# Scaling attention A's probabilities on GpSimd instead of DVE, in two operations for each head

## The chip, the core and the metric

The kernel runs on one core of one Trainium2 chip. The metric is the device time of one execution in microseconds (us). A core has TensorE (PE, with its weight loads as PEld), VectorE (DVE), ScalarE (ACT), GpSimd (POOL) and SyncE (SP), each with its own instruction stream that it works through in order, and 16 DMA engines.

## What is computed

Two layers of an encoder over 256 tokens of width 1024, all in float32. Each layer has three token mixers that read one common projection, and a gated MLP with a short convolution. The mixer that matters here is A, attention over all 256 tokens with 8 query heads and 2 key/value heads of width 64:

```python
q = rmsnorm(q.reshape(B, S, A_HEADS, HEAD_DIM), gq)
k = rmsnorm(k.reshape(B, S, A_KV_HEADS, HEAD_DIM), gk)
q = rope_2d(q, row, col) * (HEAD_DIM ** -0.5)
k = rope_2d(k, row, col)
s = jnp.einsum('bqkgd,bskd->bkgqs', qi, k).astype(jnp.float32)
p = jax.nn.softmax(s, axis=-1)
o = jnp.einsum('bkgqs,bskd->bqkgd', p, v)
```

The other mixers are B, average pooling over windows of 2, 4, 8 and 16 tokens minus the token itself, with a linear map, and C, attention over a neighbourhood on a grid.

## The kernel before

Every large product is made of three float32r products: each operand is split into a part `hi` and a remainder `lo`, and `mm3` (lines 204 to 206) adds hi x hi, lo x hi and hi x lo in PSUM. The weights come from HBM in chunks of 128 x 1024 (`raw`, issued by SP, line 154); ACT rounds each half chunk to `hi` (line 163) and DVE subtracts to get `lo` (line 168; GpSimd does it for some chunks of the MLP). `feed` keeps up to six split chunks ahead of TensorE.

In a layer, first the projections for A are made and q and k normed and rotated (`prep_a`). The rotation uses tables `rt` that hold cosine and sine multiplied by the gains of the q/k norm. `rope_tables` (lines 316 to 326) makes them on GpSimd: for each of the two gains two small copies (line 323) and four products of 128x64 (lines 325 and 326), so 12 instructions for a layer. The gains `gq` of layer 2 are loaded by SP (line 304). In the code `load_qk` and `rope_tables` for layer 2 are called in the middle of layer 1's MLP, but a scheduler sets the order of each engine's instructions by priority and by when it expects operands, and it has put both far earlier, into layer 1's attention.

Then the projections for B and C are computed, and the heads of A are laid between them. `attend` (line 582) makes one step of A for each block of a projection. A step n transposes the probabilities of head n-2 (`turn`, line 504), computes the scores of head n (lines 481 and 482), multiplies finished pairs of heads with v (`pv`, line 514), and after that block calls `scale` for head n. The softmax of a head h is:

- DVE takes the negated maximum over the keys, straight from PSUM (line 484), and multiplies it with the norm of q (line 485).
- ACT computes the exponentials into an SBUF tile `e` of 128 x 2 x 256, one instruction for each half of 128 queries, which also sums them (line 489).
- DVE takes the reciprocals of the two sums (line 495) and multiplies all of `e` by them (line 496).
- TensorE transposes `e` in four pieces (line 504), ACT copies the result from PSUM (line 506), and line 514 multiplies it with v.

Between the heads DVE also does the pooling sums of B (lines 609 to 621) and the weight splits (line 168). After the last head GpSimd issues 16 DMAs that spread C's values (line 672).

In the names, `w` stands for the tiles of `w2` and `w1`, `st` for small statistics, `ps` for a PSUM bank, `big` for the tiles of 128 x 1088, `y` for what the branches give. The lines that the change touches are 495 and 496:

```python
dve.reciprocal(rc, sm)
dve.tensor_tensor(e, e, rc[:, :, None].to_broadcast([128, 2, S]), op=OP.mult)
```

Of the kernel before, what the change touches and what calls it, by code (L numbers as in the profile page):

```python
# [13 lines left out]
OP = mybir.AluOpType  # L14
# [4 lines left out]
S = 256  # L19
# [56 lines left out]
def encoder(ctx: ExitStack, tc: tile.TileContext, x, norms, wall, bgate, gqk, wpool, pscale,  # L76
            rpbt, convp, rope, inv, out):
    nc = tc.nc
    pe, act, dve, pool = nc.tensor, nc.scalar, nc.vector, nc.gpsimd
# [19 lines left out]
    def st(n=1):  # L99
        return sb.tile([128, 16], FT, name="st", bufs=16)[:, :n]  # L100
# [107 lines left out]
    def split_from(o_hi, o_lo, src, scale=None):  # L208

        if scale is None:  # L210
            a = act.activation(o_hi, src, AF.Copy)
            b = dve.tensor_tensor(o_lo, src, o_hi, op=OP.subtract)  # L212
        else:
            a = act.activation(o_hi, src, AF.Copy, scale=scale)
            b = dve.scalar_tensor_tensor(o_lo, src, scale, o_hi.bitcast(FT), op0=OP.mult, op1=OP.subtract)
        return a, b
# [130 lines left out]
    for l in range(L):  # L347
# [124 lines left out]
        class AttA:  # L472
# [19 lines left out]
            def scale(self, h):  # L492
                e, sm = self.P[h]
                rc = st(2)
                dve.reciprocal(rc, sm)
                dve.tensor_tensor(e, e, rc[:, :, None].to_broadcast([128, 2, S]), op=OP.mult)

            def turn(self, h):
                e, _ = self.P.pop(h)
# [457 lines left out]
```

## Time and profile before

| | before |
|---|---|
| median of 3 runs | 830.1 us (829.84 to 830.25) |
| profiled execution | 830.15 us |
| its span, first to last instruction | 828.1 us |
| PE busy | 813.2 us (98%) |
| PEld busy | 708.7 us (86%) |
| DVE busy | 598.8 us (72%) |
| ACT busy | 505.4 us (61%) |
| POOL busy | 109.1 us (13%) |
| granted TensorE clock, mean | 0.998 |

The profile is of one execution. Its busy times are sums over the whole span; a wait is idle time of an engine, put down to what ended it; the timeline gives each engine's instructions in order of time, in us from the start of the span, and puts equal neighbours together. A duration there runs until the result is written, so that neighbours on an engine overlap by some hundredths of a microsecond.

### The profile page before, as it was taken

The page shows a single profiled execution, that of the slowest core. Times are in us where ns is not written, and L with a number is a line of the kernel's source. Part 1 is how long each engine was busy: PE and PEld are TensorE (multiplying, and loading weights), DVE is VectorE, ACT ScalarE, POOL GpSimd, SP SyncE. Part 2 cuts the span into 40 slices and gives each one's busy share as a digit, 9 for nine tenths or more (in the row PEclk, how much of TensorE's full clock was granted, in tenths as well). Part 3 has the DMA queues.
Part 4 walks back from the last instruction along what each step waited for, and adds up shares of the span by engine and source line. Part 5 has one row for each costly group of instructions (what it writes and reads, how often), then busy time and mean ns, then how long its engine had stood idle before and what let it go on. Part 6 is the DMA issues. An engine that isn't in the chain of part 4 may idle for free.

```text
span 828.1 us, 13731 instructions
## 1 busy us (share of the span) xinstructions
PE 813.2 (98%) x5016; PEld 708.7 (86%) x5016; DVE 598.8 (72%) x1172; ACT 505.4 (61%) x1072; POOL 109.1 (13%) x133
## 2 busy tenths in 40 slices
PE   8999999999999999999999999999999999999997
PEld 6898787887789999999889887888787899999995
DVE  5898566776668876667689965776667598766673
ACT  6667555555558755565567765655446686556652
POOL 3221400000011212111021004000001212121100
PEclk9999999999999999999999999999999999999999
DMA  8874557566575665566356535466654746655521
GB/s 290 296 262 128 166 189 241 169 196 194 167 244 182 201 200 180 177 185 197 110 201 226 173 110 153 166 214 218 205 176 133 241 161 193 188 193 182 180 98 51
DMA packets 44580, 153.90 MB, mean 186 GB/s; under 512 B 5985, under 2 KB 6241, under 8 KB 44258
## 3 DMA queue, kind: packets, MB, share of 16 engines
q1 hardware_dynamic: 43488, 150.94, 56.1%
q0 software_dynamic: 1024, 2.10, 0.9%
q8 instruction: 39, 0.64, 0.3%
q14 instruction: 27, 0.22, 0.1%
q10 hardware_dynamic: 2, 0.00, 0.0%
HBM read 149.87 MB, written 1.05 MB: 182 GB/s over the span
## 4 chain that ended last, share of the span: by engine, by line
PE 84%; DVE 7%; issue 2%; POOL 2%; DMA 2%; ACT 2%; SPq 1%; DVEq 0%; POOLq 0%; ACTq 0%
PE ps L204 27%; PE ps L205 26%; PE ps L206 26%; DVE lo L168 2%; DMA gq<-in_gqk 1%; POOL st L223 1%; PE ps L514 1%; DVE big L250 1%; PE ps L504 1%; DVE x L270 1%; ACT hi L163 1%; PE ps L563 1%; DMA raw<-in_wall 1%; PE ps L530 1%; DVE hTlo L212 1%
## 5 line engine op out<-in xcount | busy, mean ns | idle before, releaser
L163 ACT ACTIVATE hi<-raw 128x512 fp32r<-128x512 f32 x528 | 310.8, 624 | 117.7 <-PE ps L205 43.0
L168 DVE TENSOR_TENSOR lo<-raw,hi 128x512 fp32r<-128x512 f32 x486 | 323.0, 691 | 79.6 <-ACT hi L163 77.0
L204 PE MATMUL ps<-hThi,hi 128*128 128x256 f32 x768 | 218.1, 284 | 0.0
L206 PE MATMUL ps<-hThi,lo 128*128 128x256 f32 x768 | 217.0, 283 | 0.0
L205 PE MATMUL ps<-hTlo,hi 128*128 128x256 f32 x768 | 216.9, 282 | 0.0
L204 PEld LDWEIGHTS ps<-hThi,hi 128*128 128x128 f32 x768 | 146.9, 191 | 2.3 <-issue 0.8
L205 PEld LDWEIGHTS ps<-hTlo,hi 128*128 128x128 f32 x768 | 146.9, 191 | 1.7
L206 PEld LDWEIGHTS ps<-hThi,lo 128*128 128x128 f32 x768 | 146.9, 191 | 0.0
L204 PE MATMUL ps<-hi,hThi 128*128 128x512 f32 (+1 forms) x352 | 136.5, 390 | 0.0
L205 PE MATMUL ps<-lo,hThi 128*128 128x512 f32 (+1 forms) x352 | 134.8, 385 | 0.9 <-DVE lo L168 0.8
L206 PE MATMUL ps<-hi,hTlo 128*128 128x512 f32 (+1 forms) x352 | 134.9, 385 | 0.4 <-DVE hTlo L212 0.4
L204 PE MATMUL ps<-hi,y 128*128 128x512 f32 x272 | 108.7, 399 | 0.0
L205 PE MATMUL ps<-lo,y 128*128 128x512 f32 x272 | 107.6, 395 | 0.0
L206 PE MATMUL ps<-hi,y 128*128 128x512 f32 x272 | 107.6, 395 | 0.0
L168 POOL TENSOR_TENSOR lo<-raw,hi 128x512 fp32r<-128x512 f32 x42 | 55.9, 1352 | 238.1 <-ACT hi L163 238.1
L205 PEld LDWEIGHTS ps<-lo,hThi 128*128 128x128 f32 x352 | 67.2, 191 | 14.2 <-DVE lo L168 2.0
L206 PEld LDWEIGHTS ps<-hi,hTlo 128*128 128x128 f32 x352 | 67.1, 191 | 14.3 <-DVE hTlo L212 2.0
L204 PEld LDWEIGHTS ps<-hi,hThi 128*128 128x128 f32 x352 | 67.2, 191 | 14.0 <-issue 1.1
L833 ACT ACTIVATE w<-ps,cvp 128x256 f32<-128x256 f32 x88 | 48.2, 556 | 35.4 <-DVE w L835 35.4
L206 PEld LDWEIGHTS ps<-hi,y 128*128 128x128 f32 x272 | 51.1, 188 | 12.4
L204 PEld LDWEIGHTS ps<-hi,y 128*128 128x128 f32 x272 | 51.3, 188 | 11.8 <-issue 1.1
L834 DVE SCALAR_TENSOR_TENSOR w<-ps,cvp,w 128x255 f32<-128x255 f32 x88 | 41.8, 479 | 26.9 <-ACT w L833 26.7
(130 smaller groups left out, 840.8 us busy)
## 6 DMA issues: line engine op xcount, KB each, us to landing
raw<-in_wall SPq DMA_DIRECT2D x264, 512.0 KB, 3.9
gb<-in_bgate SPq DMA_DIRECT2D x12, 256.0 KB, 5.2
rpbt<-in_rpbt SPq DMA_DIRECT2D x2, 1024.0 KB, 6.5
gpost<-in_norms SPq DMA_DIRECT2D x4, 512.0 KB, 6.7
vb<-w POOLq DMA_DIRECT2D x32, 64.0 KB, 2.6
gpre<-in_norms SPq DMA_DIRECT2D x3, 512.0 KB, 4.3
out_x<-x SPq DMA_DIRECT2D x4, 256.0 KB, 2.0
x<-in_x SPq DMA_DIRECT2D x2, 256.0 KB, 3.2
```

Of the source, the lines that this page charges most:

```text
L163: act.activation(hi[c][:, z], raw[c][:, z], AF.Copy)
L168: (pool if lean else dve).tensor_tensor(lo[c][:, z], raw[c][:, z], hi[c][:, z], op=OP.subtract)
L204: pe.matmul(o, a[0], b[0], start=first, stop=False)
L205: pe.matmul(o, a[0], b[1], start=False, stop=False)
L206: pe.matmul(o, a[1], b[0], start=False, stop=last)
L212: b = dve.tensor_tensor(o_lo, src, o_hi, op=OP.subtract)
L223: pool.tensor_tensor(r, v, mhalf[:, :1], op=OP.pow)
L250: par["xn"] = dve.scalar_tensor_tensor(xn[:, c], xs[t][:, c], r, g[h], op0=OP.mult, op1=OP.mult)
L270: dve.scalar_tensor_tensor(xs[t][:, c], mg[:, c], r, xs[t][:, c], op0=OP.mult, op1=OP.add)
L504: pe.transpose(p3[:, k, t * 128:(t + 1) * 128], e[:, t, k * 128:(k + 1) * 128], ident)
L833: act.activation(u[:, c:c + S], p[:, c:c + S], AF.Identity, bias=cvp[:, l, j, 3:4], scale=cvp[:, l, j, 1:2])
L834: dve.scalar_tensor_tensor(u[:, c + 1:c + S], p[:, c:c + S - 1], cvp[:, l, j, 0:1], u[:, c + 1:c + S], op0=OP.mult, op1=OP.add)
```

## The change

The reciprocal stays on DVE. The multiplication of `e` becomes two GpSimd operations, one for each half of 128 queries, each with one tensor operand of 128 x 256 and one column of `rc` as the scalar of each partition. Lines from 496 on have a number one higher in the changed kernel, and the new operation is line 497.

```diff
                 e, sm = self.P[h]
                 rc = st(2)
                 dve.reciprocal(rc, sm)
-                dve.tensor_tensor(e, e, rc[:, :, None].to_broadcast([128, 2, S]), op=OP.mult)
+                for t in range(2):
+                    pool.tensor_scalar(e[:, t], e[:, t], rc[:, t:t + 1], None, op0=OP.mult)
```

The scheduler places the new operations. On GpSimd, in layer 1's attention, the order before was this (L400 belongs to `prep_a`, L323 to L326 are the rotary tables of layer 2, L672 the DMAs of C's values):

```order
L400 TENSOR_TENSOR rq<-st,mhalf 128x8
L323 COPY gq<-gq 128x2x16 x2
L325 TENSOR_TENSOR rt<-ropec,gq 128x64 x2
L326 TENSOR_TENSOR rt<-ropec,gq 128x64 x2
L323 COPY gq<-gq 128x2x16 x2
L325 TENSOR_TENSOR rt<-ropec,gq 128x64 x2
L326 TENSOR_TENSOR rt<-ropec,gq 128x64 x2
L672 DMA vb<-w_1059 32x512 x2
```

With the change the same place of GpSimd's queue reads (L497 is the scaling, one row for the two halves of a head):

```order
L400 TENSOR_TENSOR rq<-st,mhalf 128x8
L497 TENSOR_SCALAR w_680<-w_680,st 128x256 x2
L323 COPY gq<-gq 128x2x16 x2
L325 TENSOR_TENSOR rt<-ropec,gq 128x64 x2
L326 TENSOR_TENSOR rt<-ropec,gq 128x64 x2
L323 COPY gq<-gq 128x2x16 x2
L325 TENSOR_TENSOR rt<-ropec,gq 128x64 x2
L326 TENSOR_TENSOR rt<-ropec,gq 128x64 x2
L497 TENSOR_SCALAR w_730<-w_730,st 128x256 x2
L497 TENSOR_SCALAR w_787<-w_787,st 128x256 x2
L497 TENSOR_SCALAR w_848<-w_848,st 128x256 x2
```

Head 0 stands ahead of the 12 rotary instructions, heads 1 to 7 behind them and ahead of the DMAs. In layer 2 the eight heads follow each other with nothing between.

On DVE, from the reciprocal of head 0 in layer 1 on, the order before was this (L612 to L621 are the pooling sums):

```order
L495 RECIPROCAL st<-st 128x2
L484 TENSOR_REDUCE st<-ps 128x2
L496 TENSOR_TENSOR w_680<-w_680,st 128x512
L485 TENSOR_TENSOR st<-st,rq 128x2
L613 TENSOR_TENSOR big<-big 128x257
L168 TENSOR_TENSOR lo<-raw,hi 128x512 x2
L495 RECIPROCAL st<-st 128x2
L621 TENSOR_TENSOR w_924<-w_924,big 128x256
L496 TENSOR_TENSOR w_729<-w_729,st 128x512
L484 TENSOR_REDUCE st<-ps 128x2
L620 TENSOR_TENSOR w_927<-big,invc 128x256
L485 TENSOR_TENSOR st<-st,rq 128x2
```

With the change, from the same reciprocal on (the pooling sums have numbers one higher):

```order
L495 RECIPROCAL st<-st 128x2
L484 TENSOR_REDUCE st<-ps 128x2
L614 TENSOR_TENSOR big<-big 128x257
L485 TENSOR_TENSOR st<-st,rq 128x2
L168 TENSOR_TENSOR lo<-raw,hi 128x512 x2
L622 TENSOR_TENSOR w_928<-w_928,big 128x256
L495 RECIPROCAL st<-st 128x2
L621 TENSOR_TENSOR w_931<-big,invc 128x256
L621 TENSOR_TENSOR w_991<-big,invc 128x256
L622 TENSOR_TENSOR w_931<-w_931,big 128x256
L168 TENSOR_TENSOR lo<-raw,hi 128x512
L484 TENSOR_REDUCE st<-ps 128x2
```

The scalings are gone, and the pooling products have moved up into their places. TensorE's and SP's orders are the same as before, ACT's differs by one exchange of neighbours, and outside the heads of attention A DVE's is the same too.

## Rows read from the trace of the kernel before

**Rows 1.** The page, part 1: busy time, share of the span and instructions.

```profile
PE 813.2 (98%) x5016; PEld 708.7 (86%) x5016; DVE 598.8 (72%) x1172; ACT 505.4 (61%) x1072; POOL 109.1 (13%) x133
```

**Rows 2.** TensorE's waits: line, waited for: us in total, times, longest.

```profile
PE ps L504 <- DVE st L485: 2.7, 2, 1.5
```

**Rows 3.** Groups by form, DVE: count, busy us, mean ns, idle before.

```profile
L496 DVE TENSOR_TENSOR w<-w,st 128x512 f32<-128x512 f32 x16 | 11.1, 696 | 0.3
```

**Rows 4.** Timeline of DVE, layer 1: start us, us, instruction, count.

```profile
56.49 0.16 DVE L495 RECIPROCAL st<-st 128x2 f32<-128x2 f32 x1
56.56 0.67 DVE L484 TENSOR_REDUCE st<-ps 128x2 f32<-128x512 f32 x1
57.15 0.68 DVE L496 TENSOR_TENSOR w<-w,st 128x512 f32<-128x512 f32 x1
...
58.16 1.29 DVE L168 TENSOR_TENSOR lo<-raw,hi 128x512 fp32r<-128x512 f32 x2
59.36 0.16 DVE L495 RECIPROCAL st<-st 128x2 f32<-128x2 f32 x1
...
59.76 0.68 DVE L496 TENSOR_TENSOR w<-w,st 128x512 f32<-128x512 f32 x1
...
63.57 0.81 DVE L496 TENSOR_TENSOR w<-w,st 128x512 f32<-128x512 f32 x1
```

**Rows 5.** Timeline of TensorE, layer 1: transposes of heads 0, 1 and 2.

```profile
57.98 0.63 PE L504 MATMUL ps<-ident,w 128*128 128x128 f32 x4 [1.13 <-DVE st L485]
...
61.80 0.60 PE L504 MATMUL ps<-ident,w 128*128 128x128 f32 x4
...
65.59 0.60 PE L504 MATMUL ps<-ident,w 128*128 128x128 f32 x4
```

**Rows 6.** Timeline of GpSimd, layer 1: first four and last two of 12 rotary instructions.

```profile
57.81 2.70 POOL L323 COPY gq<-gq 128x32 f32<-128x32 f32 x2 [19.42 <-DMA gq<-in_gqk]
60.48 0.60 POOL L325 TENSOR_TENSOR rt<-ropec,gq 128x64 f32<-128x64 f32 x2
...
64.53 0.78 POOL L326 TENSOR_TENSOR rt<-ropec,gq 128x64 f32<-128x64 f32 x2
```

**Rows 7.** Timeline of GpSimd, start of layer 1: its own 12, first and last two.

```profile
14.93 0.35 POOL L323 COPY gq<-gq 128x32 f32<-128x32 f32 x2 [3.13 <-DMA gq<-in_gqk]
...
17.67 1.57 POOL L326 TENSOR_TENSOR rt<-ropec,gq 128x64 f32<-128x64 f32 x2
```

**Rows 8.** GpSimd's forms: ns min/median/max, L600 as a group with mean ns.

```profile
L323 POOL COPY gq<-gq x8: 203/305/1704, 14.9 to 62.6; 128x32 f32<-128x32 f32 x8
L139 POOL MEMSET klo<- x1: 529/529/529, 0.9 to 0.9; 128x512 f32 x1
L600 POOL MEMSET big<- 128x32 f32 x2 | 0.2, 124 | 7.4 <-DVE big L394 6.5 <-PE ps L405 0.8
L168 POOL TENSOR_TENSOR lo<-raw,hi x42: 1287/1302/1497, 246.8 to 787.2; 128x512 fp32r<-128x512 f32 x42
```

**Rows 9.** Timeline of DVE, layer 2: reciprocal and scaling of head 0, scaling of head 1.

```profile
461.75 0.15 DVE L495 RECIPROCAL st<-st 128x2 f32<-128x2 f32 x1
461.82 0.67 DVE L484 TENSOR_REDUCE st<-ps 128x2 f32<-128x512 f32 x1
462.41 0.68 DVE L496 TENSOR_TENSOR w<-w,st 128x512 f32<-128x512 f32 x1
...
465.28 0.68 DVE L496 TENSOR_TENSOR w<-w,st 128x512 f32<-128x512 f32 x1
```

**Rows 10.** Timeline of TensorE, layer 2: transposes of heads 0 and 1.

```profile
463.24 0.63 PE L504 MATMUL ps<-ident,w 128*128 128x128 f32 x4 [1.54 <-DVE st L485]
...
467.05 0.60 PE L504 MATMUL ps<-ident,w 128*128 128x128 f32 x4
```

**Rows 11.** Groups by form, GpSimd: the DMAs of attention C's values.

```profile
L672 POOL DMA_DIRECT2D vb<-w x32 | 17.5, 550 | 82.0 <-ACT w L668 80.9 <-DMA vb<-w 1.2
```

**Rows 12.** Stretch of layer 1's heads: length, PE, PEld, DVE, ACT, POOL busy, PEclk, DMA.

```profile
53.00:92.00 39.00, 37.87 (x264) 33.36 (x263) 31.39 (x70) 28.19 (x72) 7.50 (x12) 1.00 0.49 155
```

## The prediction

> **What bounds the kernel now.** I read the page's busy times first. TensorE is busy for 813.2 of the span's 828.1 us [rows 1], so almost all of the time is TensorE's own stream, which is in order and which the change leaves as it is. The only time that the change can give or take is what TensorE waits. So the second view is TensorE's waits: of the few it has, the largest are two before the transposes of attention A's probabilities (line 504), 2.7 us together, the longer one 1.5 [rows 2]. They are the first head of each layer. The trace names L485 as the releaser, the small DVE instruction right behind the scaling; what the transposes read is the tile that the scaling wrote.
>
> The third view is the order in time of DVE and TensorE around the heads. In layer 1 head 0's reciprocal starts at 56.49, the maximum of the next head (L484) stands between, and the scaling runs from 57.15 to 57.83 [rows 4]; the transposes start at 57.98 [rows 5], 0.15 later, which I take as the price of a hand-over. Head 1 is scaled by 60.44 and turned at 61.80: 1.36 to spare. Head 2 is scaled by 64.38 and turned at 65.59: 1.21 to spare [rows 4, 5]. In layer 2 head 0 is scaled by 463.09 and turned at 463.24, with nothing to spare; head 1 by 465.96 and 467.05, 1.09 to spare [rows 9, 10]. So a scaling that ends more than about 1.1 us later stops TensorE, and what TensorE stops for is not won back: after these heads its stream has nearly no waits that could shrink.
>
> The fourth view is GpSimd in that stretch, and it decides the case. At 57.81, when the DMA of the next layer's q/k gains lands, GpSimd begins that layer's rotary tables, and it is busy with those 12 small instructions until 65.31 [rows 6]. This is in the midst of heads 1 and 2.
>
> **The change part by part.** *Removed:* 16 DVE operations of 0.696 us, 11.1 in all [rows 3]. DVE is busy for 31.39 of the 39 us of layer 1's heads [rows 12], TensorE does not wait for DVE's weight splits there, and so this relief is worth nothing by itself. What it could bring is an earlier scaling for the two heads that TensorE waits for, below.
>
> *Added: 32 GpSimd operations of 128x256.* No row has this one. The nearest is the copy of 128x32, also with one operand of a tensor: 0.203 us at its shortest. The two sizes of memset, 124 ns for 32 and 529 for 512 elements, give 0.84 ns for each element; 224 more elements make 0.19, so 0.39 us [rows 8]. The other end is the subtraction of two tensors, 1.302 us for 512 elements, so 0.65 for half of it [rows 8]. I take 0.40, since it is one tensor and a scalar, and 0.80 for a head. The Trainium skill (GPSIMD Engine Reference, sections 3.1 and 4.1) says that operations with one input run at about the rate of the port, 1.03 cycles for each element, which makes an estimate of 0.22 us for each half; by that the sum below would be 0.36 us smaller. The trace of before has no such operation.
>
> *What GpSimd pays for DVE's neighbourhood.* The two copies at 57.81 take 2.70 us instead of some 0.4 [rows 6, 8]: while they stand there DVE runs subtractions and multiplications that read two tensors of SBUF, from L168 at 58.16 to the scaling that ends at 60.44 [rows 4], and the next pair of GpSimd instructions takes only 0.60 [rows 6], under the maximum of head 2, which reads PSUM. So GpSimd waits while DVE reads two SBUF tensors and runs freely when it does not. The first half of a scaling meets the L484 that follows the reciprocal, the second one an L168 or the like.
>
> *Moved: the place in GpSimd's queue.* The order shows head 0's halves ahead of the 12 rotary instructions in layer 1 and head 1's behind them, with every later head behind those. So head 1's scaling, which DVE did at 59.76, starts only when the tables are through. How long do they take now? At the start of layer 1 its own 12 took from 14.93 to 19.24, 4.31 us, with DVE less crowded [rows 7]; here 7.50 [rows 6]. In the changed order DVE still runs the pooling sums and the weight splits around them, but not the scalings, two of which (0.60 each from start to start) fell into this run. I take 7.5 - 1.2 = 6.3 us, so up to 57.81 + 6.3 = 64.1. Head 1 then needs 0.80, and 0.3 for a DVE operation under way: 65.2; with 0.15 for the hand-over its transposes start at 65.36 instead of 61.80. **That is 3.56 us of standing TensorE.**
>
> *The other heads.* Behind head 1 the queue has nothing but scalings. From a reciprocal to the end of the scaling DVE took 1.08 (59.36 to 60.44 [rows 4]); GpSimd takes 0.15 + 0.80 and up to two waits of 0.60, so 0.95 to 2.15, at worst 1.07 more, and the smallest spare time is 1.09: hidden. Head 0 of layer 2: the reciprocal ends at 461.90, the first half runs 462.05 to 462.45, under L484. The second half either follows at once (TensorE at 463.00, a gain of 0.24) or waits for the L168 that now starts where the scaling did, at 462.41 (463.56, a loss of 0.32) [rows 9, 10]. I take 0. Head 0 of layer 1 is the same, and its gain or loss vanishes in the longer wait for head 1. The DMAs of attention C's values stand behind the last scaling on GpSimd's queue, and waited 80.9 us for ACT's copies [rows 11]: they have time.
>
> *Sum.* 3.56 + 0 + 0, rounded to 3.5. The profiled execution took 830.15 us, 0.05 above the median of 830.1, so 830.15 + 3.5 = 833.6 us. Low end: tables at the pace of layer 1's own end at 62.12, the transposes start at 63.37, a loss of 1.57, less 0.24: 831.5; with every duration at its shortest (4 copies of 0.203, 8 products of 0.30: 3.2 us, no waits) the loss is 0.2 and the time 830.1. High end: head 0's second half is held until the next reciprocal (59.36), the tables start 2.0 later and take 7.5, the halves cost 0.65 and two waits: 69.96, a loss of 8.16, and 0.32 in layer 2: 838.6.
>
> **The rivals.** *1. The tables get through in time.* Decisive is when the 12 instructions end: by 62.5 the loss stays under 1.7 us. For it: their own durations are 3.2 us, layer 1's own took 4.3, three scalings are gone from DVE, and when TensorE stops DVE runs dry and lets GpSimd through. Against it: DVE's new order packs the pooling products closer together here. Time: 830.1 to 831.5, say 831.0, which is not slower by what can be told.
>
> *2. The clock falls in the stop.* At the heads no stop so far is longer than 1.5 us [rows 2], and the granted clock is 1.00 across the heads [rows 12]. A stop of 3.5 us or more has no row. Should the clock drop to 1.2 GHz, the products of one head (57.98 to 61.80, 3.8 us [rows 5]) would take up to twice as long: 833.6 + 3.8 = 837.4. The Trainium skill (TensorE: Matmul & The Clock Gate, Part 1) calls the lower level the default, which comes back when TensorE idles; no row here bears it out.
>
> *3. GpSimd is starved at every head.* If a half costs 0.65 and each half waits out several DVE operations, heads 1 and 2 of both layers come late by a further 1 to 2 us each: 836 to 839. Against it: from head 3 on DVE has idle time in each period, 7.6 of 39 us in all [rows 12].
>
> *4. Faster.* The two waits of 2.7 us [rows 2] could go if the scaling of both first heads came much earlier. It cannot come earlier than the reciprocal, which leaves some 0.2 each. As a case only what I overlook: 827.5 to 828.4.
>
> **How the numbers follow.** The forecast, GpSimd held up at head 1, loss of 1.7 to 5.5: 0.70. Rival 1: 0.15. Rivals 2 and 3 together: 0.12. Rival 4: 0.03. About 0.2% (1.7 us) is what a measurement of this kernel can tell from no change. So slower 0.82, same 0.15, faster 0.03. The range from 830.6 to 837.0 takes in most of rival 1, the forecast with its bounds, and half of rivals 2 and 3.
>
> **What would show it.** In the profile after: a wait of TensorE before line 505 (504 before) of about 3.5 us near 61 to 65 us, released by GpSimd, and none like it in layer 2; the tables' 12 instructions from about 57.8 to 64; 32 GpSimd operations whose shortest is near 0.40; DVE's busy time down by about 11 us; a granted clock of 1.00 from 53 to 100 us. Wrong would be: the transposes of head 1 at 62 or 63 (rival 1), waits at line 505 in several heads (rival 3), matmuls twice as far apart behind the stop (rival 2).

## The result, and the profile after

The changed kernel took **836.61 us** (median of 6 runs, 836.03 to 838.53) beside 829.97 us for the kernel before in the same session: a ratio of 1.0084, 95% interval 1.0074 to 1.0095. So it is 6.6 us slower. The profiled execution took 836.47 us with a span of 834.5 (828.1 before), so 6.4 us of span are to be found. The transposes are L505 in the changed kernel.

The page's busy times of the changed kernel, to be read against [rows 1]:

```profile
PE 816.2 (98%) x5016; PEld 711.0 (85%) x5016; DVE 590.4 (71%) x1156; ACT 506.5 (61%) x1072; POOL 140.1 (17%) x165
```

DVE has lost 8.4 us and GpSimd has gained 31, for 32 instructions. TensorE does the same 5016 instructions and is busy 3.0 us longer, which points to a slower clock; the rest of the 6.4 must be waits. TensorE's waits (line, waited for: us in total, times, longest), against [rows 2]:

```profile
PE ps L505 <- POOL w L497: 6.0, 4, 3.5
```

Four waits in place of two, 6.0 us in place of 2.7, and one of 3.5. The timeline of TensorE in layer 1 shows where, against [rows 5] (start us, us, instruction, count, idle before and its releaser):

```profile
57.75 0.33 PE L505 MATMUL ps<-ident,w 128*128 128x128 f32 x1 [0.90 <-POOL w L497]
61.62 0.90 PE L505 MATMUL ps<-ident,w 128*128 128x128 f32 x3 [3.54 <-POOL w L497]
...
67.75 0.60 PE L505 MATMUL ps<-ident,w 128*128 128x128 f32 x4
...
71.53 0.60 PE L505 MATMUL ps<-ident,w 128*128 128x128 f32 x4
```

It is head 0, not head 1. Its first piece, which reads the first half of the scaling, runs at 57.75, 0.23 earlier than before; the other three wait for the second half until 61.62 (57.98 before): **3.64 us lost**. Head 1 does not wait at all, and yet it comes 5.95 us later than before (67.75 against 61.80), so another **2.31 us** went between the two heads, where TensorE never stood still. Head 2 is 5.94 late: nothing is added behind head 1.

The 2.31 us are the clock. Windows of two microseconds (window, length, busy us of PE, PEld, DVE, ACT and POOL, granted clock PEclk, DMA share, GB/s), against [rows 12], where it was 1.00:

```profile
56.00:58.00 2.00, 1.10 (x9) 0.79 (x7) 2.00 (x7) 2.00 (x6) 1.24 (x2) 1.00 0.81 183
58.00:60.00 2.00, 0.08 (x1) 0.00 (x0) 2.00 (x7) 1.98 (x6) 2.00 (x1) 1.00 0.53 184
60.00:62.00 2.00, 0.38 (x2) 0.38 (x3) 0.86 (x2) 0.00 (x0) 2.00 (x4) 0.55 0.63 242
62.00:64.00 2.00, 2.00 (x11) 2.00 (x10) 0.59 (x1) 1.12 (x2) 2.00 (x9) 0.50 0.03 8
64.00:66.00 2.00, 2.00 (x12) 2.00 (x11) 1.97 (x6) 1.01 (x3) 2.00 (x3) 0.50 0.23 39
66.00:68.00 2.00, 2.00 (x15) 2.00 (x15) 0.27 (x2) 0.25 (x3) 2.00 (x3) 0.74 0.63 223
68.00:70.00 2.00, 2.00 (x20) 2.00 (x18) 1.15 (x2) 2.00 (x4) 0.99 (x2) 1.00 0.00 0
```

TensorE stood from 58 to 61.6, the granted clock fell to 0.50 (1.2 of 2.4 GHz) near 60, and it was back at 1.00 only near 67. In between, the products start 0.21 us apart instead of 0.12, and 11 or 12 instructions stand in a window that holds 20 at the full clock (68 to 70).

Why did the second half come so late? GpSimd (against [rows 6]) and DVE (against [rows 4]) in the changed kernel:

```profile
56.76 4.80 POOL L497 TENSOR_SCALAR w<-w,st 128x256 f32<-128x256 f32 x2 [19.09 <-DVE st L495]
61.52 0.35 POOL L323 COPY gq<-gq 128x32 f32<-128x32 f32 x2
...
63.81 1.07 POOL L326 TENSOR_TENSOR rt<-ropec,gq 128x64 f32<-128x64 f32 x2
```

```profile
56.50 0.16 DVE L495 RECIPROCAL st<-st 128x2 f32<-128x2 f32 x1
56.58 0.67 DVE L484 TENSOR_REDUCE st<-ps 128x2 f32<-128x512 f32 x1
57.16 0.42 DVE L614 TENSOR_TENSOR big<-big 128x257 f32<-128x257 f32 x1
57.50 0.15 DVE L485 TENSOR_TENSOR st<-st,rq 128x2 f32<-128x2 f32 x1
57.57 1.28 DVE L168 TENSOR_TENSOR lo<-raw,hi 128x512 fp32r<-128x512 f32 x2
58.77 0.42 DVE L622 TENSOR_TENSOR w<-w,big 128x256 f32<-128x256 f32 x1
59.11 0.16 DVE L495 RECIPROCAL st<-st 128x2 f32<-128x2 f32 x1
59.18 0.74 DVE L621 TENSOR_TENSOR w<-big,invc 128x256 f32<-128x256 f32 x2
59.84 0.42 DVE L622 TENSOR_TENSOR w<-w,big 128x256 f32<-128x256 f32 x1
60.17 0.68 DVE L168 TENSOR_TENSOR lo<-raw,hi 128x512 fp32r<-128x512 f32 x1
63.41 0.69 DVE L484 TENSOR_REDUCE st<-ps 128x2 f32<-128x512 f32 x1 [2.55 <-PE ps L482]
```

The two halves take 4.80 us together, until 61.56. The first starts under the maximum L484, which reads PSUM, and takes 0.93. The second is ready at 57.7, when DVE has begun a row of ten instructions without a gap, all but the reciprocal with two operands from SBUF. That row ends at 60.85. By the group of L497 a half costs 0.92 us where nothing stands against it:

```profile
L497 POOL TENSOR_SCALAR w<-w,st x32: 917/927/3885, 56.8 to 496.3; 128x256 f32<-128x256 f32 x32
```

Counted back from its end, 61.56, these 0.92 begin at 60.64, 0.2 us before the end of DVE's row. It reads as if the half had hardly run before. Neither ScalarE nor the DMA explains this: the first half took its plain 0.93 in the window from 56 to 58, with ACT busy for all 2.00 us and a DMA share of 0.81, while in the next window, where the second half does not come through, they stand at 1.98 and 0.53. Then DVE has nothing to do until TensorE makes new scores (2.55 us idle), so the rotary tables behind it run almost freely: 61.52 to 64.88, 3.4 us.

In layer 2 the halves are late once more, by little: head 1 is turned at 473.23 (6.18 later than in [rows 10]), and head 2 at 477.35 (470.84 before, 6.51 later), so layer 2 adds 6.51 - 5.94 = 0.57. The sum is 3.64 + 2.31 + 0.57 = 6.5, against 6.4 of span.

### The profile page after: what moved, and what is told of

It is laid out like the page before. It is cut to its first block, busy times and chain, and to the rows that moved or that the text cites. A ratio compares the mean times of both kernels' runs of the same rounds, so it can differ in the third digit from the quotient of the medians.

```text
span 834.5 us, 13759 instructions
## 1 busy us (share of the span) xinstructions
PE 816.2 (98%) x5016; PEld 711.0 (85%) x5016; DVE 590.4 (71%) x1156; ACT 506.5 (61%) x1072; POOL 140.1 (17%) x165
## 4 chain that ended last, share of the span: by engine, by line
PE 84%; DVE 7%; POOL 2%; issue 2%; ACT 2%; DMA 1%; DVEq 0%; POOLq 0%; ACTq 0%
PE ps L204 26%; PE ps L205 26%; PE ps L206 26%; DVE lo L168 3%; DVE big L250 1%; POOL st L223 1%; PE ps L515 1%; ACT hi L163 1%; POOL w L497 1%; PE ps L505 1%; DVE x L270 1%; DMA raw<-in_wall 1%; PE ps L564 1%; PE ps L531 1%; DVE hTlo L212 1%
## 5 line engine op out<-in xcount | busy, mean ns | idle before, releaser
L168 DVE TENSOR_TENSOR lo<-raw,hi 128x512 fp32r<-128x512 f32 x486 | 323.9, 692 | 87.9 <-ACT hi L163 84.0
L168 POOL TENSOR_TENSOR lo<-raw,hi 128x512 fp32r<-128x512 f32 x42 | 55.9, 1353 | 238.1 <-ACT hi L163 238.1
L223 POOL TENSOR_TENSOR st<-st,mhalf 128x1 f32<-128x1 f32 x16 | 11.4, 714 | 342.4 <-DVE st L233 342.4
```

The source lines that it names most:

```text
L168: (pool if lean else dve).tensor_tensor(lo[c][:, z], raw[c][:, z], hi[c][:, z], op=OP.subtract)
L223: pool.tensor_tensor(r, v, mhalf[:, :1], op=OP.pow)
```

## The experiments

Two theories stood after this. **Held half:** the second half of head 0 is passed over while DVE runs its row; TensorE stops and its clock falls. **Tables:** the forecast's, by which the rotary tables in front of head 1 are what costs. In all diffs the lines with - are those of the changed kernel.

### Head 0 back on DVE

```diff
-                for t in range(2):
-                    pool.tensor_scalar(e[:, t], e[:, t], rc[:, t:t + 1], None, op0=OP.mult)
+                if h == 0:
+                    dve.tensor_tensor(e, e, rc[:, :, None].to_broadcast([128, 2, S]), op=OP.mult)
+                else:
+                    for t in range(2):
+                        pool.tensor_scalar(e[:, t], e[:, t], rc[:, t:t + 1], None, op0=OP.mult)
```

> Head 0 of each layer is scaled on DVE again, in one operation as before; heads 1 to 7 stay on GpSimd. Held theory (GpSimd's operations wait while DVE reads two SBUF tensors without a pause): head 0 turns at 57.98 again, the rotary tables of layer 2 start at 57.8 under a crowded DVE and take 6 to 7.5 us, head 1 needs two halves of 0.92 behind them, so its transposes start at 66 to 68 instead of 61.80; time 834 to 838. Harmless theory (only head 0 has no time to spare): head 1 turns before 62.5, time 830 to 831. First-use theory (the first scaling that GpSimd runs twice in a row is slow by itself): tables end by 62 and a half of head 1 takes 3 to 4 us.

Measured: 836.95 us, beside 829.67 before: 1.0087 (1.0070 to 1.0104). The loss did not go; it moved to head 1. TensorE's transposes and GpSimd's queue of this run:

```profile
58.10 0.63 PE L508 MATMUL ps<-ident,w 128*128 128x128 f32 x4 [1.14 <-DVE st L485]
66.24 0.33 PE L508 MATMUL ps<-ident,w 128*128 128x128 f32 x1 [4.17 <-POOL w L500]
67.15 0.90 PE L508 MATMUL ps<-ident,w 128*128 128x128 f32 x3 [0.58 <-POOL w L500]
```

```profile
57.67 2.00 POOL L323 COPY gq<-gq 128x32 f32<-128x32 f32 x2 [19.49 <-DMA gq<-in_gqk]
...
65.26 3.64 POOL L500 TENSOR_SCALAR w<-w,st 128x256 f32<-128x256 f32 x4
```

Here DVE stays crowded, the tables take until 65.28 (7.6 us), and head 1 stands behind them: what the forecast described, with tables that take 1.3 us longer than it had them. So the two stops cover each other: without the first there is the second, somewhat longer (4.17 and 0.58 us). This run alone does not say which of them the changed kernel pays for.

### The tables moved behind the heads

```diff
                 for t in range(2):
-                    pool.tensor_scalar(e[:, t], e[:, t], rc[:, t:t + 1], None, op0=OP.mult)
+                    par["lastA"] = pool.tensor_scalar(e[:, t], e[:, t], rc[:, t:t + 1], None, op0=OP.mult)
...
-                rope_tables(l + 1)
+                with tc.issue_after(par["lastA"].ins):
+                    rope_tables(l + 1)
```

> The changed kernel, with the 12 rotary instructions of layer 2 put behind the last scaling on GpSimd's queue. TensorE's, DVE's and ScalarE's orders stay as they are. Theory of the held half (GpSimd's second half of head 0 is passed over by DVE's row of two-operand SBUF instructions, TensorE stops until about 61.6 us and its clock falls): the tables are not in the way, so the time stays at 836.0 to 837.3 us, head 0's transposes at 61.5 to 61.7, head 1's near 67.7, the clock 0.50 in between. Theory of the forecast (the tables hold up head 1): the loss goes with them, 830 to 831.5 us.

Measured: 836.69 us, beside 829.89: 1.0081 (1.0065 to 1.0096), the changed kernel's own loss.

```profile
57.36 0.33 PE L505 MATMUL ps<-ident,w 128*128 128x128 f32 x1 [0.90 <-POOL w L497]
61.23 0.90 PE L505 MATMUL ps<-ident,w 128*128 128x128 f32 x3 [3.54 <-POOL w L497]
...
67.06 0.60 PE L505 MATMUL ps<-ident,w 128*128 128x128 f32 x4
```

The stop is the same 3.54 us and the clock again 0.50 behind it (60 to 64). So in the changed kernel, as it stands, the tables cost nothing, and the forecast's theory falls for it.

### Was it the first use?

Another way to a slow second half would be that the first instructions of a kind are slow. Two of the same kind were put near the start of the kernel.

```diff
...
+    early = w1()
+    pool.memset(early, 0.0)
+    for _ in range(2):
+        pool.tensor_scalar(early, early, mhalf[:, :1], None, op0=OP.mult)
```

> The changed kernel with two more GpSimd operations of the same kind and size on a spare tile near the start, long before head 0. First-use theory: the second half of head 0 then takes 0.9 to 1.1 us, the transposes of head 0 start near 58.8, the clock stays at 1.00 and the time is 831 to 833. Held theory: the second half again takes near 3.9 us, head 0 turns near 61.6, the time is 836 to 838.

Measured: 838.64 us (one run); the two halves of head 0 take 4.81 us again and TensorE waits 3.55. All of the stretch is 1 us later than in the changed kernel. It is not the first use.

### A window in DVE's row

For head 1, DVE takes the maximum of the scores a second time, from PSUM, right behind the first; the result is not used.

```diff
                 dve.tensor_tensor(nm, nm, rq[:, h], op=OP.mult)
+                if h == 1:
+                    with urgent():
+                        dve.tensor_reduce(st(2), p3, axis=AX.X, op=OP.max)
```

> The changed kernel with one more DVE operation, a maximum straight from PSUM (0.6 us, its result unused), behind the maximum of head 1 in each layer. Held theory: GpSimd's second half of head 0 starts under it and ends near 58.7, head 0 turns near 58.8, no fall of the clock there; the tables then meet a crowded DVE, so head 1 may be late instead. First-use theory: the second half still takes near 3.9 us and head 0 turns at 61.6 or later.

Measured: 836.35 us (one run). DVE and GpSimd at head 0, and TensorE at head 1:

```profile
55.93 0.67 DVE L484 TENSOR_REDUCE st<-ps 128x2 f32<-128x512 f32 x1
56.52 0.68 DVE L488 TENSOR_REDUCE st<-ps 128x2 f32<-128x512 f32 x1
57.12 0.40 DVE L485 TENSOR_TENSOR st<-st,rq 128x2 f32<-128x2 f32 x1
```

```profile
56.12 1.83 POOL L500 TENSOR_SCALAR w<-w,st 128x256 f32<-128x256 f32 x2 [18.51 <-DVE st L498]
57.90 2.56 POOL L323 COPY gq<-gq 128x32 f32<-128x32 f32 x2
```

```profile
65.87 0.33 PE L508 MATMUL ps<-ident,w 128*128 128x128 f32 x1 [3.96 <-POOL w L500]
```

Two halves in 1.83 us, each at its own price: with 0.6 us more of an instruction that reads PSUM, nothing is held. DVE now waits for GpSimd instead, by little (its small L485 takes 0.40 in place of 0.15). The time did not fall, since with head 0 through, the tables run until 64.92 and head 1 stops for 3.96, as in the run with head 0 on DVE.

### The clock alone

In layer 1, 32 products whose result is overwritten were put in front of head 0's transposes, so that TensorE works in the stretch in which it stood.

```diff
+                if h == 0 and l == 0:
+                    for _ in range(32):
+                        pe.matmul(p[:, :S], hT["hi"][:, 0, :128], hT["hi"][:, 0], start=True, stop=True)
```

> The changed kernel with 32 extra products on TensorE ahead of head 0's transposes in layer 1, 3.8 us long, into the bank that the transposes then overwrite; nothing reads them. Clock theory (the stop lets the clock fall, and that costs 2.3 us): the granted clock stays 1.00, the products behind the transposes start 0.12 us apart, and from head 0's transposes to head 1's it takes 3.8 to 4.0 us instead of 6.1, or until GpSimd has head 1 ready; time 834 to 835. Rival (the slow products come from something else that GpSimd's or DVE's backlog does): they start 0.21 us apart all the same, 6.1 us from head 0 to head 1, time 836 to 838.

Measured: 834.75 us (one run), the clock 1.00 in every window from 56 to 68. The 32 products cover 56.73 to 60.58, about as long as the stop. TensorE's longest stop in these windows is 0.57 us, the clock did not fall, and the products behind the transposes start 0.12 us apart. So the slow products of the changed kernel come with the stop. This is no clean test of the half: DVE's order shifted too, and the second half was not held.

```profile
56.79 2.02 POOL L497 TENSOR_SCALAR w<-w,st 128x256 f32<-128x256 f32 x2 [18.37 <-DVE st L495]
```

Both halves took 2.02 us here. The second went ahead of an L168, which took 0.90 instead of 0.68, so a row is not always closed.

### One instruction for each head

```diff
-                for t in range(2):
-                    pool.tensor_scalar(e[:, t], e[:, t], rc[:, t:t + 1], None, op0=OP.mult)
+                pool.tensor_tensor(e, e, rc[:, :, None].to_broadcast([128, 2, S]), op=OP.mult)
```

> GpSimd scales each head in one instruction of two tensors (1.30 us for 512 elements in the kernel before) in place of two. It starts under the maximum L484, and there is no second instruction to be passed over. Theory of the held half: head 0 is turned by 58.2 to 59.0 us without a fall of the clock; then the tables run from about 58.5 in DVE's crowd until 65 to 66, head 1 is turned at 66 to 67 and the time is again 835.5 to 837.5. If an instruction that has begun is held as well, head 0 is turned at 60.5 or later.

Measured: 834.93 us, beside 829.89: 1.0058 (1.0044 to 1.0073), a little under the expectation.

```profile
56.82 1.04 POOL L496 TENSOR_TENSOR w<-w,st 128x512 f32<-128x512 f32 x1 [19.03 <-DVE st L495]
57.80 1.10 POOL L323 COPY gq<-gq 128x32 f32<-128x32 f32 x2
```

```profile
57.92 0.66 PE L504 MATMUL ps<-ident,w 128*128 128x128 f32 x4 [0.98 <-POOL w L496]
65.06 1.11 PE L504 MATMUL ps<-ident,w 128*128 128x128 f32 x4 [3.15 <-POOL w L496]
```

The whole head takes 1.04 us in one instruction, little more than one half of the other kind, and it starts under L484, so that head 0 is turned at 57.92, as early as before (57.98). What is left is the stop at head 1 behind the tables, with the clock at 0.50 again.

### Both suspects away

First, head 0 on DVE, the halves for the others, and the tables behind the heads: the edits of the first two experiments together.

```diff
-                for t in range(2):
-                    pool.tensor_scalar(e[:, t], e[:, t], rc[:, t:t + 1], None, op0=OP.mult)
+                if h == 0:
+                    dve.tensor_tensor(e, e, rc[:, :, None].to_broadcast([128, 2, S]), op=OP.mult)
+                else:
+                    for t in range(2):
+                        par["lastA"] = pool.tensor_scalar(e[:, t], e[:, t], rc[:, t:t + 1], None, op0=OP.mult)
...
-                rope_tables(l + 1)
+                with tc.issue_after(par["lastA"].ins):
+                    rope_tables(l + 1)
```

> Both suspects away: head 0 of each layer scaled by DVE as before, heads 1 to 7 by GpSimd, and the 12 rotary instructions of layer 2 behind the last scaling. If the held half of head 0 and the tables in front of head 1 are all there is, TensorE has no stop above 0.5 us at lines of attention A beyond those of before, the clock stays at 1.00, and the time is 829.5 to 831.2 us. If GpSimd is starved at every head (a third cause), head 1 is turned later than 62.5 us and the time is over 832.5.

Measured: 832.16 us, beside 829.89: 1.0029 (1.0019 to 1.0040). This lies between the two expectations, and the profiled run shows a third stop:

```profile
61.98 0.27 PE L508 MATMUL ps<-ident,w 128*128 128x128 f32 x1
64.35 0.55 PE L508 MATMUL ps<-ident,w 128*128 128x128 f32 x3 [2.09 <-POOL w L500]
```

Head 1's first half is in time, its second is held in the row that DVE has there (2.53 us for one half; counted back from its end it got its turn near 63.4, within the row). In this run TensorE stopped for 2.09 us, and the clock fell to 0.50 near 65.7, over 1 us after TensorE had begun again. The run shown is the slowest of seven. Three of them took 833.1 to 833.6 us at a mean granted clock of 0.996 or 0.997, the other four 831.8 to 832.2 at 0.998 or 0.999, which is the clock of the kernel before. By that the clock fell in three of the seven, and the median, 2.3 us behind the kernel before, has little of it. So a half can be held at head 1 too; the tables are not needed for that.

Then one instruction for each head, and the tables behind the heads:

```diff
-                for t in range(2):
-                    pool.tensor_scalar(e[:, t], e[:, t], rc[:, t:t + 1], None, op0=OP.mult)
+                par["lastA"] = pool.tensor_tensor(e, e, rc[:, :, None].to_broadcast([128, 2, S]), op=OP.mult)
...
-                rope_tables(l + 1)
+                with tc.issue_after(par["lastA"].ins):
+                    rope_tables(l + 1)
```

> The single GpSimd instruction for each head, and the 12 rotary instructions of layer 2 behind the last scaling: of the last run but the tables moved, so all that is left on GpSimd in the stretch is 8 instructions of 1.04 us. If the held start is what matters (an instruction that becomes ready in DVE's row of two-operand SBUF instructions waits until the row ends or a PSUM maximum comes), head 0 is turned at 57.9 and head 1's instruction, ready at 59.98 behind the reciprocal, starts with the maximum near 61.8 at the latest: turned at 61.9 to 63.0, a loss of 0 to 1.3, time 829.8 to 831.3 us. If the tables were all that stood in the way of head 1 and nothing is held, 829.7 to 830.1. If GpSimd is starved at head 1 as long as it was with halves (3.5 us), 832 to 833.

Measured: 830.98 us, beside 829.59: 1.0012 (1.0002 to 1.0021).

```profile
60.27 2.42 POOL L496 TENSOR_TENSOR w<-w,st 128x512 f32<-128x512 f32 x1 [2.05 <-DVE st L495]
```

```profile
61.10 0.68 DVE L168 TENSOR_TENSOR lo<-raw,hi 128x512 fp32r<-128x512 f32 x1
61.71 0.68 DVE L484 TENSOR_REDUCE st<-ps 128x2 f32<-128x512 f32 x1
62.31 0.93 DVE L168 TENSOR_TENSOR lo<-raw,hi 128x512 fp32r<-128x512 f32 x1
```

```profile
62.74 0.66 PE L504 MATMUL ps<-ident,w 128*128 128x128 f32 x4 [0.46 <-POOL w L496]
```

This shows the hold most plainly. Head 1's instruction is on GpSimd at 60.27, in the middle of a row of DVE, and ends at 62.69. The maximum L484 starts at 61.71; 0.98 later the instruction, which costs 1.04, is done. The L168 behind the maximum then waits for GpSimd (0.93 in place of 0.68). TensorE loses 0.46 at head 1 and 0.24 at head 0 of layer 2 (a wait of 1.78 in place of 1.54), and the clock stays at 1.00. The measured values lie within those expected of the held start, and it is the best form of scaling on GpSimd that was run: still 1.4 us behind the kernel before; the interval just leaves out no difference, and the size is within the 0.2% that the prediction called the limit of what can be told.

### Halves on DVE

```diff
                 nm = st(2)
-                dve.tensor_reduce(nm, p3, axis=AX.X, op=OP.max, negate=True)
+                with tc.issue_after(self.last.ins) if h == 1 else nullcontext():
+                    dve.tensor_reduce(nm, p3, axis=AX.X, op=OP.max, negate=True)
...
                 for t in range(2):
-                    pool.tensor_scalar(e[:, t], e[:, t], rc[:, t:t + 1], None, op0=OP.mult)
+                    self.last = dve.tensor_scalar(e[:, t], e[:, t], rc[:, t:t + 1], None, op0=OP.mult)
```

> No GpSimd: DVE does the two halves, each with one tensor and a column, behind the reciprocal, and for head 1's maximum that stood ahead of head 0's scaling it is put behind it. No tables in the way, no held half. If a half costs DVE 0.35 us or less and nothing but one pooling sum (0.42) stands ahead, head 0 is turned at 57.5 to 57.9 instead of 57.98, and the time is 829.0 to 830.2 us (0 to 0.9 under the kernel before); if a half costs 0.5 or more, 829.9 to 831.

Measured: 829.64 us, beside 829.89: 0.9999 (0.9990 to 1.0008). A half costs DVE 0.34 us at its shortest, against 0.92 on GpSimd, and head 0 is turned at 57.24 instead of 57.98, earlier than expected; against the kernel before this is no difference that can be told. No run is faster than the kernel before by more than the noise.

### Prices on GpSimd

24 more instructions of six kinds (and a memset before them) in layer 1's attention C, four of each, on a tile that nothing reads.

```diff
+        if l == 0:
+            spare = w2()
+            pool.memset(spare, 0.0)
+            for _ in range(4):
+                pool.tensor_scalar(spare[:, :256], spare[:, :256], mhalf[:, :1], None, op0=OP.mult)
+                pool.tensor_scalar(spare[:, :256], spare[:, :256], 0.5, None, op0=OP.mult)
+                pool.tensor_scalar(spare[:, :32], spare[:, :32], mhalf[:, :1], None, op0=OP.mult)
+                pool.tensor_scalar(spare, spare, mhalf[:, :1], None, op0=OP.mult)
+                pool.tensor_copy(spare[:, :256], spare[:, 256:])
+                pool.tensor_tensor(spare[:, :256], spare[:, :256], spare[:, 256:], op=OP.mult)
```

> The changed kernel with 24 more GpSimd instructions in layer 1's attention C, where nothing waits for them, to read prices: four each of a tensor by a column (128x256, 128x512, 128x32), a tensor by a constant (128x256), a copy (128x256) and two tensors (128x256). If a column as the scalar is what is dear, the constant takes about 0.4 us at its shortest and the column 0.92; if every instruction of one tensor and a scalar is dear, both take 0.92; 128x32 then tells the price for each element and the fixed part. The copy should take about 0.39, by the forecast's working. The time says little: 836 to 839 us.

Measured, the groups of these lines (ns at the shortest, median and longest):

```profile
L682 POOL TENSOR_SCALAR w<-w,mhalf x4: 921/922/1812, 108.7 to 127.6; 128x256 f32<-128x256 f32 x4
L683 POOL TENSOR_SCALAR w<-w x4: 849/850/879, 109.8 to 129.5; 128x256 f32<-128x256 f32 x4
L684 POOL TENSOR_SCALAR w<-w,mhalf x4: 358/362/1352, 110.7 to 130.5; 128x32 f32<-128x32 f32 x4
L685 POOL TENSOR_SCALAR w<-w,mhalf x4: 1562/1566/2582, 111.2 to 130.9; 128x512 f32<-128x512 f32 x4
L686 POOL COPY w<-w x4: 397/646/932, 112.8 to 132.6; 128x256 f32<-128x256 f32 x4
L687 POOL TENSOR_TENSOR w<-w x4: 727/896/1060, 113.3 to 133.6; 128x256 f32<-128x256 f32 x4
```

The copy takes 0.40 at its shortest, beside the 0.39 that the forecast had worked out. The scaling is another kind: 0.92, a constant hardly less (0.85). From 32 to 256 to 512 elements it is 0.36, 0.92 and 1.56 us, so 2.5 ns for each element and 0.28 at the start. At the shortest it is dearer than a multiplication of two tensors of the same size (0.73). The time, 843.1 us (one run), is outside what was expected: TensorE waited 4.1 us for DVE's scaling in attention C and its clock fell there too, in an order of DVE that had shifted; this was not followed further.

## Why the prediction was right, and where it was not

The sign was right, and the range held the time. The likeliest time, 833.6, was 3.0 too low, and the stop was not where the sum had put it. That the time came out within the range is in good part luck: the stop that the sum priced, head 1 behind the tables, did not occur, and another one of nearly the same length, 3.54 us at head 0, stood in its place. Of the signs named, 3.5 us of waiting released by GpSimd near 61 and no such stop in layer 2 came true. A shortest half near 0.40, a clock of 1.00 throughout and 11 us less of DVE's busy time did not; that time fell by 8.4, in the main because each scaling gone frees only 0.60 us from start to start (9.6 for 16) and the weight splits took 0.9 longer. By its steps:

- **Nothing won on DVE:** right. DVE's relief shortened no wait of TensorE that matters.
- **A half costs 0.40 us:** wrong, it is 0.92. The copy came out as worked out, but the scaling is not of the copy's kind, and lies outside both bounds (0.39 to 0.65). The Trainium skill (GPSIMD Engine Reference, sections 3.1 and 4.1) puts instructions with one input at about the rate of the port, 1.03 cycles an element, from which the forecast estimated 0.22 us for 256 elements. The copy agrees: from 0.20 us for 32 elements to 0.40 for 256 it grows by 0.9 ns an element, 0.23 us for 256. The scaling with a column does not (2.5 ns, 0.64 us): the measurement decides.
- **GpSimd waits while DVE reads two SBUF tensors:** right as a mechanism, and its size was off. Each half was given waits of up to 0.60; the second half of head 0 waited some 2.9 us (57.7 to 60.64), past seven DVE instructions that started in that time. One of them is the reciprocal at 59.11, which reads one small operand; the high end of the forecast let the half go at the reciprocal, but it was through only at 61.56.
- **Head 0 of layer 1, "its gain or loss vanishes in the longer wait for head 1":** this is the step that failed. The held half stood only in the high end, and the sum took it as nothing because head 1 was to wait longer anyway; head 0 lost 3.64 us, and 2.31 more by the clock, before head 1 came up. With a first half of 0.92 the second is ready at 57.7, within the row; with one of 0.40 it would have been ready at 57.16, just as the row begins, and what would have come of that no run shows.
- **6.3 us of tables in front of head 1, 3.56 of standing TensorE:** they took 3.4 us and cost nothing. That is what rival 1 had in its favour, that DVE runs dry when TensorE stops; only it was head 0's stop that made it dry. Where head 0 is in time, the forecast's stop is there: 4.17, 3.96 and 3.15 us in three runs.
- **Rival 2, the clock:** it was part of the likeliest course and not beside it. After the stop of 3.5 us (and in an experiment after one of 2.1) the clock stood at half; this cost 2.31 us, not the 3.8 allowed at most, as it recovered before the head was through. The rule of the Trainium skill that was named there (TensorE: Matmul & The Clock Gate, Part 1), that the lower level comes back when TensorE idles, is borne out by the windows above.
- **Rival 3, starvation at every head:** not at every head; the stops are at heads 0 and 1, where DVE's rows are long. From head 2 on TensorE waits for no scaling in layer 1.
- **Layer 2:** 0.57 in place of 0.

## What to carry to other kernels

A stop of TensorE has two prices, the stop and the slower clock behind it: here 3.64 and 2.31 us. Work that is given to GpSimd beside a busy DVE should be one instruction for each hand-over, placed where DVE reads PSUM or has a gap, since each further instruction can be held for as long as DVE's row lasts; and the kind must be priced by its own row, not by a copy. When one late thing is cured and the time stays, look for a second that the first had covered: here, with head 0's half cured alone, 7.3 us of loss stayed, and with the tables moved alone 6.8 (the first two runs above); with both cured it was 2.3.

## What was not expected of the hardware

- A GpSimd instruction of 0.92 us took 3.88, while seven DVE instructions in a row started ahead of it. It got its turn near the row's end; in the run with one instruction and late tables it was with the maximum from PSUM. The other way round DVE waited 0.25 us for GpSimd (L485 0.40 in place of 0.15, L168 0.93 in place of 0.68). The Trainium skill (SBUF — State Buffer, "Who interferes with whom") says that a DVE instruction with two SBUF inputs contends with a GpSimd instruction that reads SBUF, over ports that the two engines share, and that issue order decides who blocks. The rows agree that the two wait for each other. By issue order alone the half, ready at 57.7, would not have stood behind seven instructions that DVE started later, so there the rows do not bear it out.
- It is not every boundary: with the 32 products a half went ahead between two L168, and so it did in layer 2 of the changed kernel (both halves of head 0 in 1.96 us from 467.48, the second L168 0.90 in place of 0.68); both times the small L485 stood between the two L168. The tables pushed in between pooling sums in several runs (5.3 to 7.6 us instead of 3.4). Which boundary lets GpSimd in stays open.
- On GpSimd one multiplication of 128x512 by a broadcast tensor took 1.04 us, the same work as two halves by a column 1.84, and one instruction by a column 1.56.
